# A weight-streaming decoder layer: q and k weights in row blocks that alternate with v, sums of squares by products, another order on VectorE

## Chip, cores, metric

One core of one Trainium2 chip runs the whole kernel. The metric is the device time of one execution in microseconds, the median of the runs shown.

## What is computed

One layer of a decoder on 256 tokens of width 1024, in float32. Cut to what matters here:

```python
mod = silu(c) @ W_mod + b_mod            # shift1, scale1, gate1, shift2, scale2, gate2
h   = RMSNorm(x) * (1 + scale1) + shift1
z   = h @ W_in                           # q, k, v, g_dn, r, conv_b, conv_c, conv_h, gate_a, gate_c
o   = gated linear attention(q, k, v, log_sigmoid(g_dn @ gate_w2 + gate_b) / 16)   # chunks of 64
o   = per_head_rmsnorm(o) * silu(r)
u   = causal_conv3(conv_c * conv_h)
y   = (sigmoid(gate_a) * (o @ W_A) + sigmoid(gate_c) * ((conv_b * u) @ W_B)) @ W_out
x   = x + gate1 * y
x   = x + gate2 * MoE(RMSNorm(x) * (1 + scale2) + shift2)     # 64 experts, top 2 of one of 8 groups
out = RMSNorm(x)
```

All 64 experts' weights are streamed, whoever is chosen. The kernel reads 476 MB in all.

## The kernel before

The first part, the mixer, works through 88 **weight blocks** of 128 x 1024 values (512 KB), numbered `b` in the list `items`. Each is loaded into one of 12 places of a ring, together with blocks of the modulation's weights. ScalarE makes a rounded high half of a weight block (`split_h`, L302), VectorE subtracts to get the low half (`split_l`, L309), both into one of six slots `sp(b)`; the activations `h` are split in the same way (`hl`). PE then does three passes (high x high, high x low, low x high; `PASSES`) in fp32r, accumulating in PSUM. `split_h(b + 5)` stands in ScalarE's program at block `b`; it overwrites the slot of block `b - 1`, so it waits until PE is done with that block.

Order: the weights of v for input rows 0 to 511 in four blocks (128 rows each, all 1024 columns), then q and k for these rows in four blocks (512 rows by 256 columns each), then the same for rows 512 to 1023; these are blocks 0 to 15. Then r, conv's c, h and b, the two output gates a and g, and the three square matrices (A, C, O), eight blocks each, every block 24 products of 256 columns. A v block is 12 products of 512 columns (`mm_v`, L335), a q or k block 24 of 256 (`mm_half`, L326).

For each 128 input rows `h_mod(k)` needs two modulation blocks (`mod_blk`, L224: a product with silu(c) on VectorE with a sum along the row) and the normalised x (`xnorm`, L243). The norm's sum of squares is made ahead of that: squares on VectorE and ScalarE, three additions on VectorE over the eight row tiles (L268), then one product per 128 tokens with a column of ones (L271).

The work of each engine besides this is laid down by block number: `at(b, f)` runs `f` in block `b` ahead of its products, `first(b, f)` at the block's start, `pre(b, f)` between `split_h` and `split_l`. `MODS` gives the blocks at which the other 32 modulation blocks are multiplied. PSUM has four banks for the accumulators of v and of the pairs of blocks from 16 on (`zt`, tags Z0 to Z3, taken in turn; the gate takes three of them too) and four for q, k and attention (`mt`, M0 to M3). When a pair of blocks is done, `evac` empties its bank: r's and c's pairs five blocks later.

After the mixer come the router and 16 groups of four experts, each 12 units of 2 MB. A unit is loaded by SP into any slot that falls free, in a fixed order: mixer tiles such as T10 and T11 fall free on the way (`st.free`), and SP's queue waits for each.

```python
    def zt(*shape):
        i = rot["z"] % 4
        rot["z"] += 1
        return pz.tile([128, *(shape or (2, TOK))], F32, name="z", tag=f"Z{i}")
```

Of the kernel before, what the change touches and what calls it, by code (L numbers as in the profile page):

```python
# [20 lines left out]
H = 4  # L21
# [9 lines left out]
WARM = (4, 2)  # L31
XS = 38
# [6 lines left out]
CB, CN1, CN2, CGG, CCW, CGB, NCOL = 0, 48, 56, 64, 72, 96, 100  # L39
# [56 lines left out]
def trunk_kernel(ctx: ExitStack, tc: tile.TileContext, xT: bass.AP, c: bass.AP, modw: bass.AP,  # L96
# [33 lines left out]
    worder = ["v0", "v1", "q", "k", "r0", "r1", "c0", "c1", "h0", "h1", "b0", "b1",  # L130
# [12 lines left out]
    for j in range(len(items) + LA):  # L143
        if j < len(items):
            kind, n, i = items[j]
            if kind[0] == "v":
                o = 2 * (kind == "vB")
# [25 lines left out]
    crow = e11[0:1, 3072:4096]  # L173
    nc.sync.dma_start(crow, bass.AP(tensor=c.tensor, offset=c.offset, ap=[[D, 1], [1, D]]))
# [16 lines left out]
    G.iota(jp, pattern=[[1, 128]], base=0, channel_multiplier=-1)  # L191
    onesf = sm.tile([128, 128], F32, name="onesf")
# [11 lines left out]
    onesb = sm.tile([128, 128], BF, name="onesb")  # L204
    V.memset(onesb, 1.0)
# [38 lines left out]

    def h_mod(k):
        i, b = k // 4, k % 4
        if k > 0:
            mod_blk(2 * i, b)
            mod_blk(2 * i + 1, b)
# [9 lines left out]

    for i in range(2):  # L260
# [5 lines left out]
    S.activation(dum, epsc, AF.Sqrt)  # L266
# [5 lines left out]
    rc = sm.tile([128, TT], F32, name="rc")  # L272
    S.activation(rc, ps[:, :, 0], AF.Sqrt, bias=epsc, scale=1.0 / D)
# [4 lines left out]
    mod_blk(0, 0)  # L278
# [5 lines left out]
    S.copy(rstd1, pr1[:, :TOK])  # L284
    mod_blk(1, 0)
# [35 lines left out]
    def mm_half(b, kind, i, pb):  # L321
        t = sp(b).rearrange("p s (j k m) -> p s j k m", j=2, k=4)
        for j in range(2):
            for k in range(4):
                for n, (ws, rs) in enumerate(PASSES):
                    T.matmul(pb[i % 2][:, j], t[:, ws, j, k], hl[rs][:, k + 4 * (i // 2)],  # L326
                             start=(kind[1] == "A" and j == 0 and k == 0 and n == 0),
                             stop=(kind[1] == "B" and j == 1 and k == 3 and n == 2), skip_group_check=True)

    def mm_v(b, kk, pv):  # L330
        t = sp(b)
        for tt in range(TT):
            for n, (ws, rs) in enumerate(PASSES):
# [5 lines left out]
    def prep(b):  # L339

        kind, n, i = items[b]
        k = 4 * (kind == "vB") + i
        if kind[0] == "v":
            h_mod(k)
        if b > 0:
            split_l(b - 1)
        split_h(b)
        if kind[0] == "v":
            if k < KT - 1:
                xnorm(k + 1)  # L350
            h_lo(k)

# [16 lines left out]
    L["o"] = hf  # L369
# [159 lines left out]
    def o_split(h, f):  # L529
        if f is put_h and h == 0:  # L530
            L["ohl"] = big.tile([128, 2, KT, TOK], F32R, name="ohl", tag="T10")
# [3 lines left out]
    def conv_tap0(s):  # L535
        for k in range(s.start, s.stop):
            S.activation(L["cu"][:, 1, k], L["cu"][:, 0, k], AF.Identity, scale=colt[:, CCW + 16 + k:CCW + 17 + k])

    def conv_taps(s):
        for k in range(s.start, s.stop):  # L540
            u, t = L["cu"][:, 0, k], L["cu"][:, 1, k]
# [17 lines left out]
    at(1, small_loads)  # L559
    at(12, late_loads)  # L560
# [7 lines left out]
    first(16, gate2)  # L568
    first(17, gate3)
    at(17, gate4)  # L570
    at(18, gate6)
    first(19, gate5)
    first(20, gate8)
    at(20, gate7)
    at(20, lambda: k_evac(0))
    at(21, lambda: k_evac(1))
    at(22, lambda: q_evac())
    at(22, gla_setup)
    at(24, gla_kst)
    at(25, gla_attn)  # L580
    first(25, gla_kst2)
    pre(26, gla_attn2, 0)
    pre(26, gla_attn2, 1)
    at(26, gla_state, 0, 1)
    first(27, gla_state2, 0)
    pre(27, gla_state2, 1)
    at(28, gla_state, 2)
    pre(29, gla_state2, 2)
    at(30, gla_o, 0)
    at(30, gla_o, 1)  # L590
# [663 lines left out]
```

## Time and profile before

| | us |
|---|---|
| median of 3 runs | 1225.88 (1224.78 to 1226.55) |
| the profiled execution | 1227.17 |
| its span, first to last instruction | 1225.50 |
| PE busy | 899.9 (73%) |
| VectorE (DVE) busy | 380.1 (31%) |
| ScalarE (ACT) busy | 224.2 (18%) |

The busy shares are means over two stages with different limits. The engines run side by side, each in its own order, and a wait shows as idle time with the name of what ended it. PEld is PE's weight load, which overlaps its products. L numbers are lines of the kernel before.

### The profile page before, as it was taken

The numbers are of one execution on the slowest core, as the hardware profiler recorded it, in microseconds if no ns is written. First come the engines' busy times: TensorE is split into PE (matmuls) and PEld (weight loads), VectorE is DVE, ScalarE is ACT, GpSimd is POOL, SyncE is SP. The second block draws the span as 40 slices with busy tenths as digits, with TensorE's granted clock in tenths as the row PEclk, the third lists the DMA queues.
The fourth block names the chain that finished last, engine by engine and source line by source line (L and its number), as shares of the span: only waits on it lengthen the run. The fifth ranks groups of instructions, "written<-read, shape, count | busy, mean of one in ns | idle before, by whom it ended". The sixth has DMA issues, their size and how long they took to land.

```text
span 1225.5 us, 14584 instructions
## 1 busy us (share of the span) xinstructions
PE 899.9 (73%) x6175; PEld 476.2 (39%) x6175; DVE 380.1 (31%) x717; ACT 224.2 (18%) x375; POOL 4.0 (0%) x15
## 2 busy tenths in 40 slices
PE   6999999999788757675657566666656665757565
PEld 3999999998333212121212121212212111412112
DVE  7969799654412202020102111111112000302003
ACT  5674555434211000010101010101000000100002
POOL 0000000000000000000000000000000000000000
PEclk9999999999889888698988898988889888978888
DMA  9978869977999999999999999999999999999996
GB/s 363 406 235 288 274 186 341 348 270 291 398 406 428 427 427 427 428 430 428 428 427 427 427 429 427 427 428 427 428 428 428 428 427 428 425 428 427 428 425 248
DMA packets 51338, 477.84 MB, mean 390 GB/s; under 512 B 5954, under 2 KB 6082, under 8 KB 27076
## 3 DMA queue, kind: packets, MB, share of 16 engines
q1 hardware_dynamic: 50402, 475.82, 94.8%
q8 instruction: 50, 0.82, 0.3%
q10 hardware_dynamic: 866, 1.04, 0.2%
q14 instruction: 20, 0.16, 0.0%
HBM read 475.79 MB, written 1.05 MB: 389 GB/s over the span
## 4 chain that ended last, share of the span: by engine, by line
DMA 67%; PE 28%; DVE 3%; ACT 1%; issue 1%; SPq 0%; DVEq 0%; ACTq 0%
DMA unit<-in_ew_dram 53%; PE z L318 17%; DMA ring<-in_ew_dram 13%; PE a L991 3%; PE m L326 2%; PE z L335 1%; PE m L963 1%; DMA ring<-in_modw_dram 1%; PE m L1018 1%; PE a L1133 0%; PE m L486 0%; DVE xt L224 0%; PE m L482 0%; PE m L463 0%; DVE sp L309 0%
## 5 line engine op out<-in xcount | busy, mean ns | idle before, releaser
L991 PE MATMUL a<-unit,xt 128*32 128x512 f32 x1424 | 204.6, 705 | 98.2 <-DMA unit<-in_ew_dram 97.7
L991 PE MATMUL a<-unit,gt 128*32 128x512 f32 x672 | 114.1, 815 | 67.2 <-DMA unit<-in_ew_dram 62.8
L991 PEld LDWEIGHTS a<-unit,xt 128*32 128x32 f32 x1424 | 44.0, 121 | 248.9 <-DMA unit<-in_ew_dram 131.6
L318 PE MATMUL z<-hhl,sp 128*128 128x256 f32 x1152 | 140.4, 284 | 0.0
L318 PEld LDWEIGHTS z<-hhl,sp 128*128 128x128 f32 x1152 | 138.8, 192 | 1.1 <-issue 0.7
L967 ACT ACTIVATE xt<-m,modc,A 128x128 f32<-128x128 f32 x64 | 25.8, 454 | 535.3 <-PE m L963 535.3
L991 PE MATMUL a<-ring,xt 128*32 128x512 f32 x624 | 90.4, 705 | 44.8 <-DMA ring<-in_ew_dram 44.8
L309 DVE TENSOR_TENSOR sp<-ring,sp 128x1024 fp32r<-128x1024 f32 x88 | 106.6, 1221 | 47.2 <-ACT sp L302 40.0
L302 ACT CAST sp<-ring 128x1024 fp32r<-128x1024 f32 x88 | 90.8, 1047 | 96.3 <-PE z L318 69.2
L1019 DVE TENSOR_TENSOR wk<-wk,m 128x512 f32<-128x512 f32 (+2 forms) x68 | 44.5, 656 | 199.5 <-PE m L1018 199.5
L1009 DVE TENSOR_TENSOR xt<-a,xt 128x1024 f32<-128x1024 f32 (+3 forms) x19 | 20.0, 1055 | 270.8 <-PE a L991 264.0
L991 PEld LDWEIGHTS a<-unit,gt 128*32 128x32 f32 x672 | 22.2, 131 | 146.7 <-DMA unit<-in_ew_dram 93.1
L963 PEld LDWEIGHTS m<-Pm,wk 128*128 128x128 f32 x512 | 60.2, 196 | 21.7 <-issue 21.7
L963 PE MATMUL m<-Pm,wk 128*128 128x128 f32 x512 | 63.8, 283 | 5.0 <-DVE Pm L956 4.7
L1018 PE MATMUL m<-xt,pwt 128*128 128x512 f32 (+2 forms) x136 | 62.5, 601 | 5.2 <-DVE xt L1009 5.2
L999 DVE TENSOR_TENSOR gt<-gt,a 128x512 f32<-128x512 f32 x16 | 11.0, 689 | 175.0 <-ACT gt L998 175.0
L991 PE MATMUL a<-ring,gt 128*32 128x512 f32 x288 | 42.6, 718 | 28.7 <-DMA ring<-in_ew_dram 28.7
L224 DVE SCALAR_TENSOR_TENSOR xt<-ring,xt 128x1024 f32<-128x1024 f32 x48 | 58.6, 1220 | 0.6
L991 PEld LDWEIGHTS a<-ring,xt 128*32 128x32 f32 x624 | 18.2, 119 | 102.5 <-DMA ring<-in_ew_dram 63.1
L969 DVE TENSOR_SCALAR xt<-m,A,modc 128x128 f32<-128x128 f32 x64 | 23.3, 406 | 109.7 <-PE m L963 109.7
L1018 PEld LDWEIGHTS m<-xt,pwt 128*128 128x128 f32 x136 | 25.1, 199 | 48.1 <-issue 36.4
L998 ACT ACTIVATE gt<-a 128x512 f32<-128x512 f32 x16 | 9.6, 597 | 184.9 <-PE a L991 184.9
(249 smaller groups left out, 622.9 us busy)
## 6 DMA issues: line engine op xcount, KB each, us to landing
unit<-in_ew_dram SPq DMA_DIRECT2D x131, 2048.0 KB, 39.1
ring<-in_ew_dram SPq DMA_DIRECT2D x54, 2048.0 KB, 39.1
ring<-in_win_dram SPq DMA_DIRECT2D x88, 512.0 KB, 7.0
ring<-in_modw_dram SPq DMA_DIRECT2D x48, 512.0 KB, 6.3
ring<-in_ew_dram SPq DMA_DIRECT2D x12, 512.0 KB, 6.1
unit<-in_el_dram SPq DMA_DIRECT2D x4, 1024.0 KB, 34.3
unit<-in_el_dram SPq DMA_DIRECT2D x4, 512.0 KB, 18.7
ring<-in_el_dram SPq DMA_DIRECT2D x4, 512.0 KB, 12.5
```

The costliest lines, as they stand in the source:

```text
L224: V.scalar_tensor_tensor(scr, st.block("m", i, b), 1.0, cB, op0=OP.mult, op1=OP.mult, accum_out=modc[:, 4 * i + b:4 * i + b + 1])
L302: S.copy(sp(b)[:, 0], st.block("w", n, i))
L309: V.tensor_sub(t[:, 1], st.block("w", n, i), t[:, 0].bitcast(F32))
L318: T.matmul(ps, t[:, ws, k], rhs[rs][:, k], start=(clear and k == 0 and n == 0), stop=(k == KT - 1 and n == 2), skip_group_check=True)
L326: T.matmul(pb[i % 2][:, j], t[:, ws, j, k], hl[rs][:, k + 4 * (i // 2)], start=(kind[1] == "A" and j == 0 and k == 0 and n == 0), stop=(ki ...
L963: T.matmul(ps[:, j], h2[:, tt, f:f + 128], Pm[:, tt], start=(tt == 0), stop=(tt == 1))
L967: S.activation(xg[:, k], ps[:, j], AF.Identity, bias=B2[:, k:k + 1], scale=A2[:, k:k + 1])
L969: V.tensor_scalar(xg[:, k], ps[:, j], A2[:, k:k + 1], B2[:, k:k + 1], op0=OP.mult, op1=OP.add)
L991: T.matmul(ps[32 * j:32 * j + 32, 512 * hh:512 * hh + 512], lhsT[:, 32 * j:32 * j + 32], w[:, j, 512 * hh:512 * hh + 512], start=first, st ...
L1009: V.tensor_mul(X["y"][:, c0:c1], ps[:, c0:c1], X["g2r"][:, c0:c1])
L1018: T.matmul(ps[:, :w], pwt[:, tt], X["y"][:, s], start=True, stop=True)
L1019: V.tensor_add(acc[:, tt, s], acc[:, tt, s], ps[:, :w])
```

## The change

q and k are laid out like v: one block holds 128 input rows of all their 1024 columns, and blocks alternate v, q and k, v, q and k. `mm_qk` adds each into four banks, `mm_v` goes pass by pass over both token halves. c comes in with the small column table, is activated there, and eight products with the identity spread it over the partitions. The three additions of the squares are replaced by 16 products that accumulate. `start_warm` adds 16 products of a constant in five places at the start. In `prep` the high half comes first, the low half of a v block directly after h's low half. The gate's and attention's steps stand three blocks later by number, `MODS` doesn't change. conv's c blocks stand ahead of r's, and both are evacuated as soon as their pair is done. Tiles: conv's products use the storage of h and of the attention's keys, o that of the keys, the split o takes T11 in place of T10.

```diff
+START = (5, 1, 1, 3, 6)
-    for half, vn in (("A", "v0"), ("B", "v1")):
-        items += [("v" + half, vn, i) for i in range(4)]
-        items += [(n + half, n, i + 2 * (half == "B")) for n in "qk" for i in range(2)]
-    for n in worder[4:]:
+    for k in range(KT):
+        items += [("v", f"v{k // 4}", k % 4), ("qk", f"qk{k // 4}", k % 4)]
+    for n in worder[6:8] + worder[4:6] + worder[8:]:
         items += [(n[0], n, i) for i in range(4)]
...
-    nc.sync.dma_start(crow, bass.AP(tensor=c.tensor, offset=c.offset, ap=[[D, 1], [1, D]]))
...
+    onesb = sm.tile([128, 128], BF, name="onesb")
+    V.memset(onesb, 1.0)
+    cold = zt(512)
+
+    def start_warm(i):
+
+        for _ in range(START[i]):
+            T.matmul(cold, onesb, onesb[:, None, :].to_broadcast([128, 4, 128]), start=True, stop=True)
+
+    start_warm(0)
...
+    def mods(k):
+        for i in range(2):
+            mod_blk(2 * (k // 4) + i, k % 4)
...
+    S.activation(ccs, colt[:, CC:CC + KT], AF.Silu)
+    S.activation(dum, epsc, AF.Sqrt)
+    pc = [mt(4, 128) for _ in range(2)]
+    for k in range(KT):
+        T.matmul(pc[k // 4][:, k % 4], ccs[:, k:k + 1].to_broadcast([128, 128]), ident, start=True, stop=True)
     for i in range(2):
-        ps = mt()
-        T.matmul(ps, onesf[0:1, :], crow[:, 512 * i:512 * i + 512], start=True, stop=True)
-        S.activation(cB[:, 512 * i:512 * i + 512], ps, AF.Silu)
+        S.copy(cB[:, 512 * i:512 * i + 512], fl(pc[i]))
...
-    for n in (4, 2, 1):
-        V.tensor_add(xnt[:, 0:n], xnt[:, 0:n], xnt[:, n:2 * n])
-    ps = mt(2, 256)
-    for tt in range(TT):
-        T.matmul(ps[:, tt, 0:1], xnt[:, 0, 128 * tt:128 * tt + 128], onec, start=True, stop=True)
...
+    ps = mt(2, 256)
+    for k in range(KT):
+        if k % 4 == 0:
+            start_warm(1 + k // 4)
+        for tt in range(TT):
+            T.matmul(ps[:, tt, 0:1], xnt[:, k, 128 * tt:128 * tt + 128], onec, start=(k == 0 and tt == 0),
+                     stop=(k == KT - 1), skip_group_check=True)
+    start_warm(3)
+    rc = sm.tile([128, TT], F32, name="rc")
+    S.activation(rc, ps[:, :, 0], AF.Sqrt, bias=epsc, scale=1.0 / D)
+    mods(0)
...
+    start_warm(4)
...
+    def mm_qk(b, kk):
+        t = sp(b).rearrange("p s (h m) -> p s h m", h=2 * H)
+        for n, (ws, rs) in enumerate(PASSES):
+            for h in range(2 * H):
+                pb = (pq, pk)[h // H][h % H // 2]
+                T.matmul(pb[:, h % 2], t[:, ws, h], hl[rs][:, kk],
+                         start=(kk == 0 and h % 2 == 0 and n == 0),
+                         stop=(kk == KT - 1 and h % 2 == 1 and n == 2), skip_group_check=True)
...
-        for tt in range(TT):
-            for n, (ws, rs) in enumerate(PASSES):
+        for n, (ws, rs) in enumerate(PASSES):
+            for tt in range(TT):
...
+        k = b // 2
+        split_h(b)
+        if b % 2 == 0:
+            if k > 0:
+                mods(k)
             h_mod(k)
-        if b > 0:
-            split_l(b - 1)
-        split_h(b)
-        if kind[0] == "v":
-            if k < KT - 1:
-                xnorm(k + 1)
+            if k > 0:
+                split_l(b - 1)
+                if k < KT - 1:
+                    xnorm(k + 1)
             h_lo(k)
+            split_l(b)
+            if k == 0:
+                S.copy(rstd1, pr1[:, :TOK])
+                xnorm(1)
...
-    first(12, lambda: v_evac())
-    at(13, gate0)
-    first(14, gate0b)
-    at(14, gate1, 0)
-    at(14, gate1, 1)
-    first(15, gate_abs)
-    pre(15, gate_min)
...
+    at(8, small_loads)
+    at(14, late_loads)
+    first(15, lambda: v_evac())
+    at(16, gate0)
+    first(17, gate0b)
+    at(17, gate1, 0)
+    at(17, gate1, 1)
+    first(18, gate_abs)
+    pre(18, gate_min)
+    first(19, gate2)
+    first(20, gate3)
+    at(20, gate4)
...
+    at(25, lambda: q_evac())
+    at(25, gla_setup)
+    at(27, gla_kst)
+    at(28, gla_attn)
+    first(28, gla_kst2)
+    pre(29, gla_attn2, 0)
+    pre(29, gla_attn2, 1)
+    at(29, gla_state, 0, 1)
...
-    L["o"] = hf
+    L["o"] = gb[:, 2:4].rearrange("p a h t -> p (a h) t")
...
-    def conv_setup():
-        L["cu"] = big.tile([128, 2, KT, TOK], F32, name="cu", tag="T11")
+    cu0 = hf
+    cu1 = gb[:, 0:2].rearrange("p a h t -> p (a h) t")
...
-            pre(b + 5, r_evac, q, ps)
+            pre(b, r_evac, q, ps)
         elif kind == "c":
-            if q == 0:
-                pre(b + 5, conv_setup)
-            pre(b + 5, c_evac, s, ps)
+            pre(b, c_evac, s, ps)
```

## Rows read from the trace of the kernel before

**Rows 1.** The page's 40 slices of 30.6 us: what the loads moved.
```profile
GB/s 363 406 235 288 274 186 341 348 270 291 398 406 428 427 427 427 428 430 428 428 427 427 427 429 427 427 428 427 428 428 428 428 427 428 425 428 427 428 425 248
```

**Rows 2.** The chain that ended last: start us, us, engine and line, number of instructions.
```profile
17.93 1.14 DVE sp L309
...
27.66 4.83 PE z L335 x20
32.48 11.51 PE m L326 x96
44.00 10.91 PE z L335 x48
...
57.77 1.00 PE z L378 x16
...
61.84 1.73 PE z L388 x8
...
69.32 23.04 PE z L318 x192
92.36 0.87 PE m L438 x8
...
96.10 1.79 PE m L451 x16
...
100.75 1.93 PE m L463 x16
...
383.18 28.19 DMA unit<-in_ew_dram
```

**Rows 3.** Timeline of VectorE: start us, us, line, operation, count.
```profile
8.28 2.41 DVE L268 TENSOR_TENSOR t<-t 128x1024 f32<-128x1024 f32 x3 [1.13 <-ACT t L265]
...
15.44 1.22 DVE L224 SCALAR_TENSOR_TENSOR xt<-ring,xt 128x1024 f32<-128x1024 f32 x1
...
19.70 1.22 DVE L224 SCALAR_TENSOR_TENSOR xt<-ring,xt 128x1024 f32<-128x1024 f32 x1
```

**Rows 4.** Timeline of PE at the start; in brackets the idle time before.
```profile
10.74 1.02 PE L271 MATMUL m<-onesf,t 128*128 128x1 f32 x4 [4.49 <-DVE t L268]
...
16.06 2.08 PE L335 MATMUL z<-sp,hhl 128*128 128x512 f32 x4 [2.99 <-ACT sp L302]
19.12 7.88 PE L335 MATMUL z<-sp,hhl 128*128 128x512 f32 x24 [0.98 <-DVE sp L309]
```

**Rows 5.** Timeline of ScalarE, at the start, near 66 us and near 128 us.
```profile
13.38 0.39 ACT L250 ACTIVATE A<-modc,b,colt 128x1 f32<-128x1 f32 x1
...
14.66 0.40 ACT L255 CAST hhl<-t 128x256 fp32r<-128x256 f32 x1
...
18.93 0.41 ACT L255 CAST hhl<-t 128x256 fp32r<-128x256 f32 x1
...
66.36 1.05 ACT L302 CAST sp<-ring 128x1024 fp32r<-128x1024 f32 x1 [1.91 <-PE m L326]
67.31 1.57 ACT L397 ACTIVATE t<-z,ngb 128x256 f32<-128x256 f32 x4
...
128.41 0.59 ACT L666 COPY cu<-z 128x512 f32<-128x512 f32 x1 [3.62 <-PE m L486]
```

**Rows 6.** Timeline of VectorE, 92 to 100 us.
```profile
92.50 1.28 DVE L670 SCALAR_TENSOR_TENSOR gb<-m,t 128x512 f32<-128x512 f32 x2
...
98.25 1.35 DVE L455 COPY_PREDICATED gc<-cmask,m 128x512 f32<-128x512 int32 x2
```

**Rows 7.** Busy time by stretch: PE, PEld, DVE, ACT, POOL (instructions), granted clock, DMA share, GB/s.
```profile
69.30:298.00 228.70, 228.70 (x1913) 226.54 (x1911) 169.66 (x230) 111.33 (x143) 0.96 (x1) 1.00 0.80 277
...
341.20:344.50 3.30, 1.61 (x14) 0.73 (x16) 1.82 (x6) 0.68 (x2) 0.00 (x0) 1.00 1.03 437
344.60:354.80 10.20, 8.10 (x40) 2.12 (x36) 0.69 (x1) 1.18 (x2) 0.00 (x0) 0.50 0.98 384
378.80:382.10 3.30, 3.30 (x24) 0.73 (x19) 0.00 (x0) 0.00 (x0) 0.00 (x0) 0.50 0.99 422
```

More of the change, by code (lines that the diff above doesn't have):

```diff
@@ L127, in fl @@
         return t.rearrange("p a b -> p (a b)")
-    worder = ["v0", "v1", "q", "k", "r0", "r1", "c0", "c1", "h0", "h1", "b0", "b1",
+    worder = ["v0", "v1", "qk0", "qk1", "r0", "r1", "c0", "c1", "h0", "h1", "b0", "b1",
               "a0", "a1", "g0", "g1", "A0", "A1", "C0", "C1", "O0", "O1"]
@@ L145, in trunk_kernel @@
             kind, n, i = items[j]
-            if kind[0] == "v":
-                o = 2 * (kind == "vB")
+            if kind == "v":
+                o = 2 * int(n[1:])
                 blocks += [(("m", o, i), modw[o, :, 1024 * i:1024 * i + 1024]),
@@ L530, in o_split @@
         if f is put_h and h == 0:
-            L["ohl"] = big.tile([128, 2, KT, TOK], F32R, name="ohl", tag="T10")
+            L["ohl"] = big.tile([128, 2, KT, TOK], F32R, name="ohl", tag="T11")
         f(L["ohl"], L["o"][:, 2 * h:2 * h + 2], slice(2 * h, 2 * h + 2))
@@ L557, in pre @@
         todo.setdefault((i, "pre"), []).append((f, a))
-    at(1, small_loads)
-    at(12, late_loads)
-    first(12, lambda: v_evac())
-    at(13, gate0)
-    first(14, gate0b)
-    at(14, gate1, 0)
-    at(14, gate1, 1)
-    first(15, gate_abs)
-    pre(15, gate_min)
[L568 to L590, printed above, removed]
-    first(31, gla_o2, 0)
-    first(31, gla_o2, 1)
-    at(31, gla_o, 2)
-    at(31, gla_o, 3)
-    first(32, gla_o2, 2)
-    first(32, gla_o2, 3)
-    at(33, gla_ss)
-    first(34, gla_ss2)
-    pre(35, gla_ss3)
-    at(36, gla_ss4)
+    at(8, small_loads)
[10 more added lines that the diff above has]
+    at(20, gate4)
+    at(21, gate6)
+    first(22, gate5)
+    first(23, gate8)
+    at(23, gate7)
+    at(23, lambda: k_evac(0))
+    at(24, lambda: k_evac(1))
+    at(25, lambda: q_evac())
[6 more added lines that the diff above has]
+    at(29, gla_state, 0, 1)
+    first(30, gla_state2, 0)
+    pre(30, gla_state2, 1)
+    at(31, gla_state, 2)
+    pre(32, gla_state2, 2)
+    at(33, gla_o, 0)
+    at(33, gla_o, 1)
+    first(34, gla_o2, 0)
+    first(34, gla_o2, 1)
+    at(34, gla_o, 2)
+    at(34, gla_o, 3)
+    first(35, gla_o2, 2)
+    first(35, gla_o2, 3)
+    at(36, gla_ss)
+    first(37, gla_ss2)
+    pre(38, gla_ss3)
+    at(39, gla_ss4)
     for h in range(H):
-        at(38 + 2 * h, o_norm, h)
-        at(40 + 2 * h, o_split, h, put_h)
-        at(41 + 2 * h, o_split, h, put_l)
+        at(40 + 2 * h, o_norm, h)
+        at(42 + 2 * h, o_split, h, put_h)
+        at(43 + 2 * h, o_split, h, put_l)
     for b, ms in mod_at.items():
@@ L661, in trunk_kernel @@
     ps = None
-    def conv_setup():
-        L["cu"] = big.tile([128, 2, KT, TOK], F32, name="cu", tag="T11")
+    cu0 = hf
+    cu1 = gb[:, 0:2].rearrange("p a h t -> p (a h) t")
     def c_evac(s, ps):
-        S.copy(L["cu"][:, 0, s], ps)
+        S.copy(cu0[:, s], ps)
     def q_evac():
@@ L685, in b_high @@
         s = slice(2 * q, 2 * q + 2)
-        put_h(L["chl"], L["cu"][:, 1, s], s)
+        put_h(L["chl"], cu1[:, s], s)
     def b_low(q):
         s = slice(2 * q, 2 * q + 2)
-        put_l(L["chl"], L["cu"][:, 1, s], s)
+        put_l(L["chl"], cu1[:, s], s)
         if q == 3:
-            st.free("T11")
+            st.free("T10")
     def v_evac():
@@ L702, in evac @@
     def evac(b, kind, n, i, ps):
-        if kind[0] in "vqk":
+        if kind in ("v", "qk"):
             return
@@ L734, in evac @@
             if q == 3:
-                st.free("T10")
+                st.free("T11")
         elif kind == "C":
@@ L770, in trunk_kernel @@
     for b in range(LA, nb):
-        if items[b][0][0] not in "vqk":
+        if items[b][0] not in ("v", "qk"):
             ahead.setdefault(b - (LA if b // 2 <= XS + 2 else LA - 2), []).append(b)
     for b, (kind, n, i) in enumerate(items):
-        if i % 2 == 0 and kind[0] not in "vqk":
+        if i % 2 == 0 and kind not in ("v", "qk"):
             ps = (zt(), zt()) if n == "O1" and i == 2 else zt()
         nxts = ahead.get(b, ())
-        early = b + LA < nb and items[b + LA][0][0] in "vqk"
+        early = b + LA < nb and items[b + LA][0] in ("v", "qk")
         run((b, "first"))
@@ L790, in trunk_kernel @@
         run(b)
-        if kind[0] == "v":
-            mm_v(b, 4 * (kind == "vB") + i, pv)
-        elif kind[0] in "qk":
-            mm_half(b, kind, i, pq if kind[0] == "q" else pk)
+        if kind == "v":
+            mm_v(b, b // 2, pv)
+        elif kind == "qk":
+            mm_qk(b, b // 2)
         else:
```

46 lines of the change are left out of this document (11 added, 35 removed).

## Prediction

> **What bounds the kernel now.** I read the page's table of slices first, then the chain of waits, then the timelines of single engines. The slices [rows 1] show two regimes. From the third to the eleventh the loads run at 186 to 398 GB/s, and PE is busy all of 69.3 to 298 us [rows 7]; from the thirteenth on the loads stand near 427 GB/s, all but the last slice. The chain [rows 2] says the same in order of time: from 27.66 us on it is PE alone, block after block, and from 383.18 us it is loads. A load into a slot can only be issued when a block has used the slot up, so in the first regime every load waits for PE's progress; the stream of the second regime follows on that. So I take a microsecond that PE gains or loses in the first regime as a microsecond of the end, one for one. Only the front, 0 to about 130 us, is changed.
>
> In that front, blocks 0 to 15 (v, q, k) are 96 products of 512 columns at 10.91/48 = 0.227 us and 192 of 256 columns at 11.51/96 = 0.120 us [rows 2]: 21.8 + 23.0 = 44.8 us. They take from 16.06 us [rows 4] to 69.32, less 1.00 and 1.73 for the gate's products between them: 50.5 us. So 5.7 us are lost after the first product, and 16.06 us before it. The loss is fed by VectorE: one v block takes it 15.44 to 19.70 = 4.26 us [rows 3]: two modulation products, 15.44 to 17.93, so 1.25 each; a low-half subtraction, 1.14 [rows 2]; small ones, for 12 x 0.227 = 2.7 us of PE, while the q and k blocks that would fill PE come only after four v blocks.
>
> **The new start.** The three additions, 2.41 us [rows 3], go; 16 products with one column take their place, each in two records. Of these the trace has four records in 1.02 us, 0.255 each [rows 4]; that was at the lower clock level, since the first 512-column products right after took 2.08/4 = 0.52 us against 0.227 later (1.2 against 2.4 GHz, though the clock column reads 1.00 there). Bounds for the 32 records: 8.2 us at the lower level, 4.1 at the upper. Half of them run before the second half of the squares is there (ScalarE, about 8.5 us), so at the upper level they end near 10.6 and at the lower 4.1 later. I take the upper, because the warm-up products and the eight that spread c keep PE at work from about 1.2 to 6.8 us, and in the trace the switch came inside the 24 products that start at 19.12 and take 7.88 us, between 24 x 0.227 and 24 x 0.52.
>
> From 10.6: root, reciprocal, transposes and the normalising product take about 1.6 us, to 12.2. Block 0's high half on ScalarE (1.05 us, from about 11) is now ahead of the modulation and ends at 12.0; two small activations to 12.7, then 0.63 and 0.41 for h and its high half (in the trace 13.38 to 15.06 for the four [rows 5]). The first v product can start at 13.8, 2.3 us earlier. The 4 KB load of c, gone from SP's queue, lets all loads start 0.4 us earlier; that is in these times.
>
> **The alternating blocks.** VectorE then does h's low half, block 0's low half and the next normalisation (0.35 + 1.14 + 0.37) and starts modulation 1 at 15.6. Its period for 128 rows is the old 4.26 plus one more subtraction: 5.40 us. PE's is 12 x 0.227 + 24 x 0.120 = 5.60. The loads' is four blocks of 0.524 MB at the 406 GB/s of the second slice [rows 1]: 5.2 us. PE is the slowest by little. In detail: v0 13.8 to 16.5; qk0's first two passes to 18.4; its third waits for the low half at 15.6 + 2.4 + 1.14 = 19.2, and ends at 20.15; the next h is there 3.9 us after modulation starts (15.44 to 19.34 [rows 3, 5]), at 19.5. From there PE runs through: 20.15 + 7 x 5.60 = 59.4, against 69.32 - 2.73 = 66.6. **Gain 7.2 us.**
>
> **What the gate costs, moved behind block 15.** In the four-bank ring of accumulators, blocks 16 and 17 take a bank, the gate's three tiles take the other three, and block 18 needs the first again. Its copy-out (c's) is queued on ScalarE in block 18 behind the high half of block 23, which itself waits until PE has finished block 17, and behind four Relus of the gate. By the trace: 66.36 to 67.31 for the high half, 1.57 for the Relus, 0.59 for the copy [rows 5]: PE stands 3.1 us. Before, the gate took its banks during q and k, which use none of this ring, and r's copies came five blocks later. Without this stall block 18 would wait for nothing else. **Loss 3.1.**
>
> **The list MODS is not moved.** q's evacuation ended at 93.7 [rows 6], 7.1 us after PE began its block 22 (69.32 + 6 x 2.88, from 23.04/8 [rows 2]). To the masked copies of block 26 VectorE had three subtractions and one modulation, 3 x 1.14 + 1.25 = 4.7 us; PE had four blocks and the gate's products, 4 x 2.88 + 0.87 + 1.79 = 14.2. So it came 7.1 + 4.7 - 14.2 = 2.4 us early: 98.25 against 100.68 [rows 2, 6]. Now these steps are blocks 25 to 29, and blocks 26 to 28 hold five modulations: 9.7 us. With the same lag (the gate's chain on ScalarE and VectorE is the same) the first copy starts 2.6 us late, takes 0.66, and the state products, which write the same banks, have 0.24 us to do before (1.93/8 [rows 2]): PE stands 2.6 + 0.66 - 0.24 = 3.0 us. Below a lag of 4.1 us nothing is lost; at 8 us 3.9. The last state that block 33 reads comes after three more subtractions, seven modulations and five state products, 3.4 + 8.8 + 2.0 = 14.2 us, PE's way there is 4 x 2.88 + 1.93 + 1.5 = 14.9: just in time. **Loss 3.0.**
>
> **The clock at these two stalls.** In the front PE never stood over 1 us after 19.12 [rows 4], and the clock column stays at 1.00 to 298 [rows 7]. Later, after PE sat idle half of 341.2 to 344.5, the granted clock was 0.50, that is 1.2 GHz, from 344.6 to 354.8; another such spell ran 378.8 to 382.1 [rows 7]. A spell of 3.3 us at half speed costs PE 1.7 us, none costs 0, one after each stall 3.4. I take one, the middle. The Trainium skill's page "TensorE: Matmul & The Clock Gate" (section "Why this matters for your kernels") tells to leave no idle gaps between bursts of matmuls, as the clock falls back after them. It speaks against this change: by it both stalls would pay, and the sum below would be 1.7 higher.
>
> **Costed at nothing.** The other order of passes and row halves in v: same count, and the low half is needed later than now. c ahead of r: same blocks, one Silu table load as before. The two conv and o tiles change places, T10 for T11: each is freed at the block where the other was (54 and 72), so SP's loads stay in their order. The small loads on ScalarE's queue, now in block 8: some 20 us before the gate reads them. c's and r's copies at once instead of five blocks later: 0.6 us each on ScalarE, busy 111 of 229 us there [rows 7]; the one that isn't covered is the one at block 18 above.
>
> **Sum.** -7.2 + 3.1 + 3.0 + 1.7 = +0.6 us. The profiled execution took 1227.17 (span 1225.50 and 1.67 around it), 1.29 above the median of 1225.88; so 1227.8 for a like execution, and 1226.5 at the median. About 0.2%, 2.5 us, is what a measurement of this kernel can tell from no change.
>
> **Rivals.**
> - VectorE keeps up (its lag at q's evacuation is under 4.1 us): no second stall and no spell there; -7.2 + 3.1 and one spell or none, -4.1 to -2.4: 1221.8 to 1223.5. For it: the immediate copies change ScalarE's order in the gate's chain. Against: the chain's lengths are the same. 0.20.
> - Neither stall, because block 18's bank is free in time: 1218.7. Against it stands the count of tiles in the ring. 0.05.
> - Slower: PE is at the lower clock when the one-column products start. They and what follows come 4.1 us later, v0 at 17.9: 1226.5 + 4.1 = 1230.6. It decides at about 7 us: if the clock is up by then, it doesn't hold. For it: these products move one column each, so that PE may look idle; against: the switch in the trace. 0.10.
> - Slower: both stalls pay a spell, and one of them lasts longer, as that of 10.2 us did [rows 7]: 1.7 for the second and up to (10.2 - 3.3)/2 = 3.4 for the length, 1228.2 to 1231.6. For it: idle shares as at 341 us; against: PE is full before and after. 0.15.
> - The forecast, both stalls with none to two short spells, -1.1 to +2.3: 1224.8 to 1228.2. 0.50.
>
> **Numbers.** Faster by over 0.2% (below 1223.4) are the second rival and most of the first, 0.22; slower (above 1228.3) the two slow ones and a tip of the forecast, 0.26; the rest, 0.52, is within. The range reaches from the first rival's end to the cold start, 1221.8 to 1230.5, and leaves out the case without stalls and the worst spells, some 0.15. The likeliest case's own range is 1224.8 to 1228.2.
>
> **What would show it.** Right: v's first product near 13.8 at 0.23 us each; PE without gaps from 20 to 59; PE idle some 3 us ahead of block 18, released by the copy of c; idle again at the state products, released by the masked copy; a half-clock stretch right behind one of them; block 16 some 7 us earlier, the loads' plateau starting where it did. Wrong: one-column products at 0.25 us a record; VectorE waiting for loads before 59 us; no gap at block 18; or a PE front that moves while the end doesn't, which would say that the first regime does not carry over one for one.

## The result, and the profile after

The changed kernel takes 1233.23 us, the median of 4 runs (1232.06 to 1234.30), against 1226.17 (1224.78 to 1226.55) for the kernel before: ratio 1.0059, 95% interval 1.0042 to 1.0077. It is slower, and outside the range that was given. The profiled execution took 1232.06 us, its span is 1230.2.

| landmark, us from the start of the span | before | forecast | after |
|---|---|---|---|
| first v product | 16.06 | 13.8 | 17.23 |
| end of blocks 0 to 15 (before: less the gate's products) | 66.6 | 59.4 | 63.08 |
| the router's first product | 306.64 | 307.2 | 311.19 |
| from there to the end of the span | 918.9 | 918.9 | 919.0 |
| end of the span | 1225.5 | 1226.1 | 1230.2 |

Of the 4.7 us between the two spans, 4.55 are there when the router starts. The timeline of PE in the changed kernel (start us, us, line, operation, count, idle time before and what ended it), with the lines that answer to [rows 2, 4]:

```profile
1.19 2.32 PE L197 MATMUL z<-onesb 128*128 128x512 bf16 x5 [1.19 <-DVE onesb L191]
5.77 3.78 PE L272 MATMUL m<-ident,ccs 128*128 128x128 f32 x16 [2.26 <-ACT ccs L268]
...
9.77 2.04 PE L286 MATMUL m<-onesf,t 128*128 128x1 f32 x16
...
11.89 1.84 PE L286 MATMUL m<-onesf,t 128*128 128x1 f32 x16
...
17.23 3.12 PE L347 MATMUL z<-sp,hhl 128*128 128x512 f32 x12
20.19 2.07 PE L338 MATMUL m<-hhl,sp 128*128 128x256 f32 x16
22.59 1.22 PE L338 MATMUL m<-hhl,sp 128*128 128x256 f32 x8 [0.33 <-DVE sp L321]
...
26.39 3.04 PE L338 MATMUL m<-hhl,sp 128*128 128x256 f32 x24
29.27 2.91 PE L347 MATMUL z<-sp,hhl 128*128 128x512 f32 x12
32.01 3.04 PE L338 MATMUL m<-hhl,sp 128*128 128x256 f32 x24
...
63.08 1.07 PE L394 MATMUL z<-t,e 128*32 128x256 f32 x16
...
74.77 27.67 PE L330 MATMUL z<-hhl,sp 128*128 128x256 f32 x216 [2.96 <-ACT t L682]
...
110.77 0.70 PE L479 MATMUL m<-t,gc 64*128 64x256 f32 x2
113.89 1.99 PE L479 MATMUL m<-t,gc 64*128 64x256 f32 x14 [2.42 <-DVE gc L471]
...
311.19 0.19 PE L901 MATMUL m<-osum,tri 128*128 128x64 bf16 x1 [1.05 <-DVE osum L897]
```

Read from the bottom, two of the steps are plain. Both stalls are where they were forecast, released by what was forecast: 2.96 us ahead of block 18, by the copy of c (L682), and 2.42 us at the state products, by the masked copies (L471). The alternating blocks also do what they should: behind the 0.33 us at 22.59 there is no idle time up to 63.08, and one pair of blocks takes 32.01 - 26.39 = 5.62 us (forecast 5.60).

What is off is the start. The 32 records of the one-column products take 2.04 + 1.84 = 3.88 us (4.1 was taken), but they begin at 9.77, and c's products, which spread it over the partitions, wait for ScalarE until 5.77. ScalarE's timeline says why:

```profile
0.87 0.41 ACTq L176 DMA_DIRECT2D colt<-in_cols_dram  x1
1.32 1.28 ACT L268 ACT_TABLE_LOAD   x1 [1.32 <-PEq L1256]
5.50 0.21 ACT L268 ACTIVATE ccs<-colt 128x8 f32<-128x8 f32 x1 [2.90 <-DMA colt<-in_cols_dram]
...
7.88 0.59 ACT L274 COPY xt<-m 128x512 f32<-128x512 f32 x1 [0.65 <-PE m L272]
9.58 0.59 ACT L274 COPY xt<-m 128x512 f32<-128x512 f32 x1 [1.12 <-PE m L272]
10.07 1.06 ACT L276 ACTIVATE t<-xt 128x1024 f32<-128x1024 f32 x1
```

It waits 2.90 us for the column table, which now carries c. The loads at the start (first when they were issued, by which engine's queue; then KB each and median us from issue to landing), first the kernel before:

```profile
0.87 0.38 ACTq L178 DMA_DIRECT2D colt<-in_cols_dram  x1
0.87 0.34 SPq L174 DMA_DIRECT2D e<-in_c_dram  x1
1.28 0.84 SPq L176 DMA_DIRECT2D xt<-in_xT_dram  x2
```

```profile
xt<-in_xT_dram SPq DMA_DIRECT2D x2, 512.0 KB, 4.6
colt<-in_cols_dram ACTq DMA_DIRECT2D x1, 50.0 KB, 1.9
```

and the changed kernel, whose table is issued at 0.87 us as well, in ScalarE's timeline above:

```profile
0.87 0.87 SPq L174 DMA_DIRECT2D xt<-in_xT_dram  x2
```

```profile
xt<-in_xT_dram SPq DMA_DIRECT2D x2, 512.0 KB, 4.4
colt<-in_cols_dram ACTq DMA_DIRECT2D x1, 54.0 KB, 4.6
```

Before, SP's queue issued the 4 KB load of c first and x at 1.28 us, 0.4 us behind the table's issue on ScalarE's queue. Now both queues issue at 0.87 us, and the table lands 2.7 us later than it did, about when x does. The Trainium skill, "DMA: Bandwidth & Descriptors", section "Queues, rings and completion order", says that each DMA engine takes turns between its queues by whole packets; the landing times agree with a table that shares the engines with x, but no run here shows the turns themselves.

The spell at half clock behind the first stall is in the busy times by stretch (columns as in [rows 7]):

```profile
75.10:78.40 3.30, 3.30 (x18) 3.30 (x17) 0.00 (x0) 1.97 (x2) 0.00 (x0) 0.50 0.93 372
78.50:102.00 23.50, 23.50 (x198) 23.50 (x197) 17.22 (x19) 17.40 (x19) 0.96 (x1) 1.00 0.51 159
```

18 records in 3.30 us against 198 in 23.50: 0.183 us each, then 0.119. Nothing like it follows the second stall. The page's row of loads has its plateau from the thirteenth slice on, as in [rows 1].

```profile
GB/s 364 367 282 281 255 170 308 381 250 289 396 404 430 426 428 429 427 428 428 427 429 427 428 427 427 428 429 427 427 429 428 427 428 428 426 427 429 428 425 245
```

### The profile page after: what moved, and what is told of

Read it like the earlier page. It is cut to its first block, busy times and chain, and to the rows that moved or that the text cites. A ratio compares the mean times of both kernels' runs of the same rounds, so it can differ in the third digit from the quotient of the medians.

```text
span 1230.2 us, 14679 instructions
## 1 busy us (share of the span) xinstructions
PE 921.4 (75%) x6231; PEld 486.6 (40%) x6231; DVE 377.9 (31%) x714; ACT 224.3 (18%) x376; POOL 4.0 (0%) x15
## 5 line engine op out<-in xcount | busy, mean ns | idle before, releaser
L1005 PE MATMUL a<-unit,xt 128*32 128x512 f32 x1424 | 214.7, 736 | 96.7 <-DMA unit<-in_ew_dram 96.2
L1005 PE MATMUL a<-unit,gt 128*32 128x512 f32 x672 | 115.6, 824 | 66.6 <-DMA unit<-in_ew_dram 61.2
L1005 PE MATMUL a<-ring,xt 128*32 128x512 f32 x624 | 86.1, 675 | 37.4 <-DMA ring<-in_ew_dram 37.4
L1005 PE MATMUL a<-ring,gt 128*32 128x512 f32 x288 | 46.9, 783 | 23.7 <-DMA ring<-in_ew_dram 23.5
```

Source lines behind the costliest of these rows:

```text
L1005: T.matmul(ps[32 * j:32 * j + 32, 512 * hh:512 * hh + 512], lhsT[:, 32 * j:32 * j + 32], w[:, j, 512 * hh:512 * hh + 512], start=first, st ...
```

## The experiments

Each ratio is to the kernel before, measured beside it, with its 95% interval. "Router" is the router's first product in the profiled execution; before it is at 306.64, in the changed kernel at 311.19.

| kernel | median us | ratio, interval | router |
|---|---|---|---|
| changed | 1233.23 | 1.0059, 1.0042 to 1.0077 | 311.19 |
| changed, again | 1234.74 | 1.0066, 1.0051 to 1.0082 | 311.06 |
| c's copy on VectorE | 1231.80 | 1.0046, 1.0033 to 1.0058 | 309.98 |
| steps three blocks later | 1228.20 | 1.0018, 1.0008 to 1.0029 | 308.62 |
| table ahead of x | 1231.05 | 1.0036, 1.0023 to 1.0049 | 308.55 |
| copy and steps | 1226.28 | 0.9999, 0.9989 to 1.0009 | 305.32 |
| steps and table | 1226.49 | 1.0003, 0.9994 to 1.0012 | 307.82 |
| all three | 1224.57 | 0.9984, 0.9975 to 0.9993 | 302.02 |
| all three, no warm-up products | 1225.89 | 0.9988, 0.9976 to 1.0000 | 306.16 |
| all three, additions again | 1224.72 | 0.9984, 0.9975 to 0.9992 | 303.61 |
| all three, 42 more products | 1232.98 | 1.0055, 1.0042 to 1.0069 | 311.63 |
| before, 42 more products | 1234.83 | 1.0069, 1.0055 to 1.0084 | 316.20 |
| changed, wait filled | 1233.14 | 1.0053, 1.0039 to 1.0068 | 311.27 |

**e1_bank: the bank of block 18 is emptied by VectorE at once.** The first of c's copies leaves ScalarE's queue.

```diff
-            pre(b, c_evac, s, ps)
+            if q == 0:
+                V.tensor_copy(cu0[:, s], ps)
+            else:
+                pre(b, c_evac, s, ps)
```

> The changed kernel, but the first pair of c is copied out of its bank by VectorE at once, ahead of its subtraction in block 18, instead of by ScalarE behind the Relus. Theory (the stall ahead of block 18, and the half-clock spell behind it, carry over to the end one for one): PE's gap ahead of block 18 falls from 3.1 to some 0.8 us, no half-clock spell follows at 75 us, and the time falls by 2.3 + 1.7 = 4.0 us, from 1233.2 to about 1229.2. Rival (the gap is absorbed later, at the state products, because VectorE is the one that is late): the gap goes but PE waits about 4 us longer at the state products, and the time stays at 1232 to 1234.

Measured: 1231.80 us. PE's timeline:

```profile
72.69 26.18 PE L330 MATMUL z<-hhl,sp 128*128 128x256 f32 x216 [0.78 <-DVE t L734]
...
107.20 0.70 PE L479 MATMUL m<-t,gc 64*128 64x256 f32 x2
111.17 3.50 PE L479 MATMUL m<-t,gc 64*128 64x256 f32 x14 [3.28 <-DVE gc L471]
```

The stall ahead of block 18 falls to 0.78 us and the spell behind it is gone: the same 216 products take 26.18 instead of 27.67 us, so a spell costs 1.5. PE now comes to the state products 3.57 us earlier (107.20 against 110.77). VectorE's masked copies come only 2.72 us earlier, first the changed kernel, then this one:

```profile
113.12 1.33 DVE L471 COPY_PREDICATED gc<-cmask,m 128x512 f32<-128x512 int32 x2
```

```profile
110.40 1.32 DVE L471 COPY_PREDICATED gc<-cmask,m 128x512 f32<-128x512 int32 x2
```

So the wait there grows from 2.42 to 3.28 us, and a half-clock spell now stands behind it (3.50 us for 14 records, not 1.99). The two stalls are coupled: of the 3.57 us, 0.86 are paid in the longer wait and 1.5 in the new spell, and 1.2 are left at the router. The theory's 4.0 us did not come, and the rival had the cause right but not the size: the wait grew by 0.86 us and not by 4, and 1231.80 lies just under its band.

**e2_mods: the modulation blocks move with the steps.** The entries 24 to 33 of the list stand three later, as the gate's and attention's steps already did.

```diff
-MODS = (19, 24, 26, 26, 27, 28, 28, 29, 29, 30, 30, 31, 31, 31, 32, 32, 33, 47, ...
+MODS = (19, 27, 29, 29, 30, 31, 31, 32, 32, 33, 33, 34, 34, 34, 35, 35, 36, 47, ...
```

> The changed kernel, but the modulations listed for blocks 24 to 33 stand three blocks later, 27 to 36, as the gate's and attention's steps do. Theory (VectorE is late at the masked copies because five modulations come before them): the wait at the state products goes and the time falls by 2.4 to 3.0 us, and by 1.7 more in executions where a half-clock spell follows that wait: 1228.5 to 1230.8. Rival (the wait moves on to conv's taps and the third state, since VectorE has the same work in fewer blocks): PE waits elsewhere between 120 and 160 us, and the time stays at 1232 to 1234.

Measured: 1228.20 us, 5.0 below the changed kernel and 0.3 below the band that the theory gave. VectorE's masked copies now start ahead of the state products, and the wait there is gone (110.70, without idle time ahead of it):

```profile
108.25 1.35 DVE L471 COPY_PREDICATED gc<-cmask,m 128x512 f32<-128x512 int32 x2
```

```profile
110.70 2.00 PE L479 MATMUL m<-t,gc 64*128 64x256 f32 x16
```

That VectorE was late because of the five modulations is shown. Of the rival's later wait there is 0.38 us, at 154.26 us. Of its profiled execution's 4.2 us of shorter span (1226.0 against 1230.2) the router shows 2.57; the other 1.6 lie behind the router, where nothing was changed, and were not traced.

**e3_table: the column table ahead of x on SP's queue.**

```diff
+    colt = sm.tile([128, NCOL], F32, name="colt")
+    nc.sync.dma_start(colt, cols)
...
-    colt = sm.tile([128, NCOL], F32, name="colt")
-    S.dma_start(colt, cols)
```

> The changed kernel, but the table with c is loaded first, on the queue of the large loads and ahead of x. Theory (the start is late because the table's packets stand behind x's, so c's products begin at 5.8 us): the table is there near 3 us instead of 5.5, c's copies end near 7 us, v's first product moves from 17.2 to about 14 and the time falls by 2.5 to 3.3 us, to 1230 to 1230.7. Rival (the start is set by the sum of squares and by PE's low clock, not by c): v's first product moves by under 1 us and the time by under 1 us.

Measured: 1231.05 us. The loads and the start:

```profile
xt<-in_xT_dram SPq DMA_DIRECT2D x2, 512.0 KB, 4.3
colt<-in_cols_dram SPq DMA_DIRECT2D x1, 54.0 KB, 2.0
```

```profile
3.29 3.67 PE L272 MATMUL m<-ident,ccs 128*128 128x128 f32 x16
...
9.10 2.05 PE L286 MATMUL m<-onesf,t 128*128 128x1 f32 x16
...
14.52 3.02 PE L347 MATMUL z<-sp,hhl 128*128 128x512 f32 x12
```

The table lands in 2.0 us again, the first v product comes 2.7 us earlier, at 14.52 (forecast for the change itself: 13.8), and all of it is kept up to the router (2.64 us). Both stalls are unchanged, 2.96 and 2.43 us. So the late table is the cause of most of the late start. Its size is not the reason, as the same 54 KB land in 2.0 us here; nor is ScalarE's queue by itself, on which the table landed in 1.9 us before. The median lies just above the theory's band of 1230 to 1230.7, and the profiled execution fell only from 1232.06 to 1231.44: its stretch behind the router is 921.1 us, 2.0 longer than in the changed kernel, though nothing was changed there.

**e4_all: the three edits together.**

> The three edits together on the changed kernel: the first pair of c copied by VectorE, the modulations three blocks later, the table first. Theory: the gains add, 4.0 + 2.7 + 2.9 = 9.6 us and up to 1.7 for a second clock spell: 1222 to 1224, under both kernels. Rival (the front's gains are partly absorbed before the loads become the limit): between 1226 and 1230.

Measured: 1224.57 us, ratio 0.9984 to the kernel before: it beats both. The router starts at 302.02, 9.2 us ahead of the changed kernel and 4.6 ahead of the kernel before, of which the median shows 2. The time lies between the theory's band (1222 to 1224) and the rival's (1226 to 1230), so the gains add at the router and only in part at the end.

**e9_bankmods and e10_modstable: the pairs.** The edits are those of above.

> The changed kernel with the steps of blocks 24 to 33 three blocks later and with c's first copy on VectorE at once, start unchanged. The first of these alone gave 1228.2 us and the router's first product at 308.6, the second alone 1231.8 with its gain given back at the state products. Theory: the two stalls are coupled through VectorE's lateness; with that gone, the copy's edit brings what it could not bring alone, the 2.2 us of idle time (2.96 to 0.78) and the 1.7 us of the half-clock spell behind it: PE is without a half-clock spell from 20 us to 300 us, the router starts at 304.7, time 1224.3 to 1225. Rival: the edit of the copy costs VectorE as much later as it saves (a 0.6 us copy on a late engine): router 307 to 308.6, time 1227 to 1228.5.

> The changed kernel with the steps of blocks 24 to 33 three blocks later and with the column table loaded first on SP's queue, c's copy unchanged. Theory of parts that add: the start's 2.6 us come on top of the 308.6 us of the steps alone, router at 306.0, gap ahead of block 18 still 2.96 us with its half-clock spell, time 1225.6 to 1226. Rival, that the start's gain is eaten before the router when the stall ahead of block 18 stays: router at 307.5 or later, time 1227 or more.

Measured: 1226.28 and 1226.49 us. With the steps moved, the copy's edit is worth 3.66 us from the gate's first product to the router (63.37 to 305.32 here, 63.01 to 308.62 without it): all that it could not bring alone, as the theory of coupled stalls said (3.9). The router (305.32, theory 304.7) bears it out; the time lies between the theory's band and the rival's, as does that of the other pair. There the start's edit brought less than it did alone, as the rival had it at the router (307.82), but for a reason that neither theory nor rival had and that the clock gives. The start of the pair of steps and table:

```profile
9.52 3.41 PE L286 MATMUL m<-onesf,t 128*128 128x1 f32 x16
...
16.31 3.04 PE L347 MATMUL z<-sp,hhl 128*128 128x512 f32 x12
```

The second half of the one-column products takes 3.41 us, against 1.84 in the changed kernel, at a granted clock of 0.50 from 8.9 to 15.7 us; with the table's edit alone that spell is 3.4 us long and begins at 10.6, when these products are nearly done. This is like the forecast's cold start, for a part of the products, except that the clock had been up before and fell: the first half of the same products took 2.05 us. It costs 16.31 - 14.52 = 1.8 us. Behind the gate's first product nothing of it changed (245.54 us to the router, 245.61 with the steps alone).

**e5_nowarm: all three edits without the 16 warm-up products.**

```diff
-START = (5, 1, 1, 3, 6)
+START = (0, 0, 0, 0, 0)
```

> The kernel with all three edits (1224.6) without any warm-up product, so that PE starts on c's products cold. Theory A (the warm-ups bring the clock up before v's first products): c's products, those of the squares and v's first block run at the lower level, v's first block takes over 5 us instead of 2.9, and the time rises by 2 to 4 us, to 1226.5 to 1228.5. Theory B (they mainly stand ahead of the transposes and of v in PE's order, and VectorE's period leaves PE no way to use an earlier start): within 1 us of 1224.6. Theory C (they cost): the transposes come 0.5 us earlier and the time falls by up to 1 us.

```profile
7.08 6.98 PE L286 MATMUL m<-onesf,t 128*128 128x1 f32 x32 [0.35 <-DVE t L275]
...
16.95 3.35 PE L347 MATMUL z<-sp,hhl 128*128 128x512 f32 x7 [1.65 <-ACT hhl L262]
```

The 32 records take 6.98 us instead of 3.79 (1.95 and 1.84 with the warm-up), and the first v products 3.35/7 = 0.48 us each: the lower level, though the clock column reads 1.00 in this stretch. All twelve of that block take 5.13 us, over 5 as theory A had it, and the router comes 4.1 us later. At the end the 2 to 4 us of theory A do not show: 1225.89 us is 1.3 above the kernel with all three edits, but the two were measured at different times, and the ratios to the kernel before (0.9988 and 0.9984) differ by 0.5 us, with intervals that overlap.

**e6_adds: all three edits, with the three additions on VectorE and two products instead of 16.**

```diff
-    for k in range(KT):
-        if k % 4 == 0:
-            start_warm(1 + k // 4)
-        for tt in range(TT):
-            T.matmul(ps[:, tt, 0:1], xnt[:, k, ...], onec, start=(k == 0 and tt == 0), ...)
+    for n in (4, 2, 1):
+        V.tensor_add(xnt[:, 0:n], xnt[:, 0:n], xnt[:, n:2 * n])
+    start_warm(1)
+    start_warm(2)
+    for tt in range(TT):
+        T.matmul(ps[:, tt, 0:1], xnt[:, 0, ...], onec, start=True, stop=True)
```

> The kernel with all three edits (1224.6), but with the three additions on VectorE and two products in place of the 16 products of the squares. Theory (the products take the additions' 2.4 us off the path): the root comes 1.5 to 2.5 us later and the time rises by as much, to 1226 to 1227. Rival (16 products at 0.11 to 0.25 us a record cost as much as they save): within 0.7 us of 1224.6.

Measured: first v product at 15.77 instead of 14.22, router 1.6 us later, the median not told apart (1224.72, where the theory had 1226 to 1227). The sum of squares by products is worth 1.6 us of the start and nothing that can be measured at the end.

**e8_extra and e11_extra2: 42 products more ahead of block 20**, in the kernel before and in that with all three edits.

```diff
+                if b == 20:
+                    for _ in range(42):
+                        T.matmul(fl(ps), onesb, onesb[:, None, :].to_broadcast([128, 4, 128]), start=True, stop=True)
```

> The kernel before, with 42 products of a constant (512 columns, bf16) ahead of block 20's products; the result is overwritten. They hold PE for 42 x 0.216 = 9.1 us without letting it stand. Theory (a microsecond of PE in the first regime is one of the end): the time rises by 8.5 to 9.5 us, to 1235.2 to 1236.2, and the router begins 9.1 us later. Rival (the loads' stream takes up part, since slots fall free that the loads were not ready for): the router begins 9 us later, but the time rises by 3 to 7 us only.

> The kernel with all three edits (1224.6 us, router's first product at 302.0) with 42 constant products of 512 columns added ahead of block 20, which cost 9.56 us of PE in the kernel before. Theory, that the end follows what PE has done by the router: router at 311.6, nearly the changed kernel's 311.2, and the time is nearly the changed kernel's too, 1232 to 1233.5. Rival, that part of a PE delay is taken up by slack behind the router (0.85 of it carried over in the kernel before): 1224.6 + 0.85 x 9.56 = 1232.7 is not told apart from that; but if the three edits left slack that the changed kernel lacks, below 1230.

Measured: the router comes 9.56 and 9.61 us later, the medians rise by 8.0 us (1226.83 to 1234.83) and 8.4 (1224.57 to 1232.98, measured at different times). The first lies between the theory's band and the rival's 3 to 7 us. A PE delay in the front carries over at 0.84 to 0.88 by these medians; the interval of the first ratio, 1.0055 to 1.0084, is 6.7 to 10.3 us and does not exclude one for one. The second kernel's router stands 0.4 us behind that of the changed kernel, and its time, 1232.98, is near the changed kernel's. That agrees with an end set by the time at which PE is through with the front. But it is not all: the kernel before with 42 products more comes to the router 5.0 us later than the changed kernel (316.20), and its 1234.83 us is hardly above the changed kernel's 1233.23 and 1234.74.

**e0_again, l1_look, l2_look, l3_look, e12_fill: why other executions are longer.** The medians of the changed kernel and the kernel before differ by 7.1 us, the profiled executions (1232.06 and 1227.17) by 4.9. The changed kernel was run again unchanged, and three more of its executions were profiled. In the last kernel PE works on constants while it waits at the state products:

```diff
+        if b == 29:
+            for _ in range(18):
+                T.matmul(ps[:, 1], onesb, onesb[:, None, :].to_broadcast([128, 2, 128]), start=True, stop=True)
         run(b)
```

> The changed kernel again, unchanged, for its spread and a second profile. Theory (each execution pays the two waits; whether a half-clock spell follows the second one, at the state products, differs from execution to execution): the median is again 1232 to 1234, and a profile that is about 2 us longer than the first one, 1232 against 1230, has a spell near 111 us where the first has none. Rival (the 2 us between executions come from the second regime): the spells of the front are the same in both profiles and the difference arises after 310 us.

> The changed kernel, unchanged, one more profiled execution. Theory: if its time is 1233.5 or more, its trace shows a half-clock spell behind the wait at the state products, near 114 us, which the two profiled executions of 1232.1 us do not have. Rival: a longer execution shows the same front and a longer stretch after the router's start (919.0 us in both).

> The changed kernel, unchanged, a second further profiled execution. Theory and rival as for the first look: in an execution of 1233.5 us or more, a half-clock spell near 114 us, or the same front and a longer stretch after the router's start.

> The changed kernel, unchanged, a third further profiled execution. Theory and rival as for the first look: in an execution of 1233.5 us or more, a half-clock spell near 114 us, or the same front and a longer stretch after the router's start.

> The changed kernel with 18 constant products of 256 columns into the empty half of block 29's own bank, right ahead of the state products, so that PE works through most of the 2.4 us in which it waited for the masked copies (18 x 0.11 = 2.0 us). Theory: in many executions a half-clock spell follows that wait, as in the profile of the kernel with c's copy on VectorE (3.4 us long, 1.7 us of loss), and makes the median some 2 us longer than the profiled execution; with PE at work the spell does not come, the state products still start near 113.9 us in the profile, and the median falls by 1 to 2 us, to 1231.5 to 1233.5 where the changed kernel gave 1233.2 and 1234.7. Rival: the longer executions are longer elsewhere; the median stays at 1233 to 1235.

Measured: the profiled executions of the changed kernel took 1232.16, 1233.55, 1231.29 and 1232.34 us, that of the kernel with the wait filled 1233.95. In none is there a half-clock spell behind the wait at the state products. The one of 1233.55 has the front of the first profile (router at 311.24) and is longer behind it, 920.3 us against 919.0. Its busy times by stretch, and then those of the first profile:

```profile
368.00:1187.90 819.90, 543.29 (x3376) 172.12 (x3372) 120.84 (x270) 44.32 (x98) 0.00 (x0) 0.85 1.01 428
```

```profile
368.00:1186.90 818.90, 550.93 (x3376) 172.49 (x3372) 120.87 (x270) 44.38 (x98) 0.00 (x0) 0.84 1.01 428
```

The same 3376 records of PE at the same 428 GB/s take 1.0 us longer, in the stretch that is bound by loads. The one of 1233.95 is longer there too: 920.7 us behind a router at 311.27. The shortest, 1231.29, has the same stall ahead of block 18, but no spell behind it:

```profile
75.23 26.18 PE L330 MATMUL z<-hhl,sp 128*128 128x256 f32 x216 [2.96 <-ACT t L682]
```

It had a spell of 6.8 us in the start instead. Filling the wait took its idle time from 2.42 to 0.43 us and changed nothing else:

```profile
110.78 2.14 PE L806 MATMUL z<-onesb 128*128 128x256 bf16 x18
112.84 0.70 PE L479 MATMUL m<-t,gc 64*128 64x256 f32 x2
113.97 1.99 PE L479 MATMUL m<-t,gc 64*128 64x256 f32 x14 [0.43 <-DVE gc L471]
```

The median, 1233.14, lies where the bands of theory and rival overlap, so it does not decide. The profiles speak against a hidden spell: the execution of 1233.55 has none and is longer behind the router, and so is the one of 1233.95, in which PE hardly waits there. But no execution above 1234 was profiled, so what lengthens the longest (up to 1237.08) stays open.

## Why the prediction was wrong

**The step that failed is the new start.** It put v's first product at 13.8 us; it came at 17.23. The working had no term for when the column table lands. It had c's products done at about 6.8 us, where they ran from 5.77 to 9.55, and counted the missing c load as a small gain: "lets all loads start 0.4 us earlier". In the changed kernel the 54 KB table, from which c now comes, starts together with two loads of 512 KB and lands after 4.6 us instead of 1.9. Loading it first brings 2.7 of the 3.4 us back; the one-column products' own time was forecast well (4.1, measured 3.88), and the cold start that was a rival did not hold in the changed kernel. That v's first product came near that rival's 17.9 is chance: it was late for another cause. The remaining 0.7 us of the start (14.52 against 13.8) are for the most part the one-column products: with the table first they end at 9.10 + 2.05 = 11.15, where the forecast had 10.6, and v's first product follows 3.37 us behind, where it had 3.2.

**What held.** The alternating blocks' 5.62 us a pair, without a wait; the stall ahead of block 18 (3.1, measured 2.96); the wait at the state products with MODS unmoved (3.0, measured 2.42); one spell at half clock behind the two stalls and not two (1.7, measured 1.5). Undoing the two stalls' causes, one each, took 2.18 of the 2.96 us and all of the 2.42 away at their places. The sum, against the profiled execution:

| term, us | forecast | measured |
|---|---|---|
| blocks 0 to 15, end against before | -7.2 | 63.08 - 66.6 = -3.5 |
| stall ahead of block 18 | +3.1 | +2.96 |
| wait at the state products | +3.0 | +2.42 |
| spell | +1.7 | +1.5 |
| rest up to the router | 0 | +1.2 |
| at the router | +0.6 | +4.6 |

So 3.7 of the 4.0 us by which the forecast missed the router are the front of blocks 0 to 15, almost all of it the start. The 1.2 us of the rest were not traced to one place; PE has no idle time in them that the kernel before does not have. A part is also there with all three edits (302.02 - 60.08 against 306.64 - 66.6 is 1.9, of which 0.78 is the idle time left ahead of block 18 and 0.38 a wait at 147.66).

**The median, a second step that failed.** The forecast took the median to lie 1.29 us below a like profiled execution, as it did before. In the changed kernel it lies 1.17 above. Of the 6.7 us by which the forecast missed the median, 4.0 are at the router and 2.5 are this step. So the late table does not explain the whole miss, and with the table first the median, 1231.05, is still above the range that was given. Of the difference between the two kernels some 0.3 us lie outside the span: every execution of the changed kernel and its variants takes 1.8 to 2.2 us there, those of the kernel before 1.6 to 1.8. That a longer stretch behind the router can make 1.3 us of such a difference is shown; the whole of it is not.

**One for one.** For a delay it is nearly so, 0.84 to 0.88, and from the changed kernel to all three edits the router moved by 9.2 us and the median by 8.7. For a gain below the kernel before the medians show less: between a router at 307.82 and one at 302.02 the time fell from 1226.49 to 1224.57, 1.9 us for 5.8. But each router time is that of one execution, and the first of these had the long spell in its start. Whether the forecast's 7.2 us would have reached the end was not tested. What takes a gain up behind the router was not settled. The stretch from there to the end is 918.9 us before and 921.3 with all three edits, with the half-clock spells at other places between 324 and 355 us; but it is 917.6 with the additions again, whose router is only 1.6 us later. In the profiled executions of the changed kernel and its variants it lies between 917.1 and 921.3 us, in no order with the router's time, so one profile cannot tell what became of 2 us.

**The rule on idle gaps.** Here the granted clock fell to 0.50 behind the 2.96 us stall in eight of nine profiled executions that had it (the exception is the one of 1231.29), and behind the second stall not once at 2.4 us in six, but once at 3.28. The Trainium skill, "TensorE: Matmul & The Clock Gate", section "Why this matters for your kernels", asks that idle gaps between bursts stay below a limit that it gives, as the clock falls back after longer ones; the prediction left the limit out. The first stall agrees with that, but for the exception; the second, half a microsecond shorter, cost its idle time alone.

## What to carry to other kernels

When a value moves into another load, price that load anew: here what started beside it decided when it landed, and a 4 KB load ahead of the big ones had kept them 0.4 us behind the table. When some entries of a list that is laid down by block number move, check the others: moving MODS after the steps gave back 2.57 us at the router and 5.0 at the median. Two stalls in a row that hang on a third engine are not priced singly: take the first away, and see how far the second grows. And a forecast from one profile to a median needs the spread: here the two lay 1.3 us apart one way before and 1.2 the other way after.

## What the runs showed of the hardware

- A 54 KB load on ScalarE's queue took 4.6 us to land when two loads of 512 KB started with it on SP's queue; ahead of them on SP's queue it took 2.0. On ScalarE's queue, issued 0.4 us ahead of them, 50 KB took 1.9. With the table first x was issued 0.45 us later and took as long to land (4.3 us, against 4.4).
- One-column products took 0.12 us a record after warm-up products and 0.22 without (3.88/32 and 6.98/32), and 0.21 at a granted clock of 0.50 (3.41/16, with steps and table).
- The start's half-clock spell changes between executions of one kernel: 3.4 us long from 13.6 in the first profile, 6.8 from 12.6 in the one of 1231.29, which then had no spell behind the stall at 75 us. In these two, as with the table ahead of x (from 10.6) and with steps and table (from 8.9), the granted clock fell while PE ran the one-column products, without idle time of PE at that point.
